# A first piece of 3584 columns with an early store of its own, in a 4-wide L2 pooling kernel

## The chip, the cores and the metric

The kernel runs on one core of a Trainium2 chip. The metric is the device time of one execution in microseconds (us). Three runs of the kernel before gave 394.51, 394.56 and 394.76 us; the median is 394.56 us.

## The reference

The input is `x` of shape 32 x 256 x 4096 in float32. Each run of four neighbours along the last axis becomes one output: the square root of the mean of the four squares.

```python
out_length = length // kernel_size          # 4096 // 4
for i in range(out_length):
    window = np.abs(x[:, :, start:end]) ** p        # p = 2, four elements
    result[:, :, i] = (np.mean(window, axis=-1)) ** (1.0 / p)
```

No output needs anything from another window, so the array can be cut anywhere at a multiple of four. 134.22 MB are read and a quarter of that, 33.55 MB, is written.

## The kernel before, in words

The flat array is seen as 128 partitions of 262144 columns. It is cut into 20 loads: 19 of `W` = 13184 columns (6.75 MB each) and a last one, load 19, of `LAST` = 11648 columns (5.96 MB). The loads are grouped into seven *blocks* (line 50). A block is a contiguous region of `x` and of `out`; inside it each partition owns one contiguous row, so that a store of a block of four loads writes 52736 contiguous bytes per partition.

Three input tiles (`x_tiles`, `X_SLOTS` = 3) are used in turn. All loads are issued by SyncE (SP) at line 83, and load i+3 is issued after the arithmetic on load i, when its tile is free again. The order of all work is written out by hand (`manual_schedule`); each engine runs its instructions in program order.

For loads 0 to 17 the work on a load is done in two halves of 6592 columns:

- ScalarE (ACT) squares the half in place (`square`, line 97).
- VectorE (DVE) adds elements 0, 1 to 2, 3 of each group (`pairs`, line 103), and then the two sums (`fours`, line 107), into a PSUM tile `st`.
- ACT takes the square root with a scale of 1/4 (`root`, line 110) into one of four slots of the output tile `ot`. Slot q holds columns qR to (q+1)R, with R = 3296.

When a block's roots are done, its slots are stored in one DMA (`store`, line 94). The stores of blocks 0 to 3 are issued on ACT's queue from `roots`; those of blocks 4, 5 and 6 are issued on SP's queue, behind all loads. So SP's queue carries all loads and the last three stores. The next roots into `ot` wait for a store of `ot` to land.

The last two loads are handled apart. Load 18 is squared partly by DVE (line 147, columns 0 to 5560) and partly by ACT (the other 7624); DVE then does pairs and fours of both parts, and ACT one root over 3296 results, after which SP stores block 5 (1.69 MB). Load 19 is taken in three pieces with the borders in `ends` (line 153): 6912, 3152 and 1584 columns. ACT's order here is: square of piece 1, root of load 18, square of piece 2, root of piece 1, square of piece 3, root of piece 2, root of piece 3. Only then does SP store block 6 (1.49 MB), the last DMA of the program. The results of loads 18 and 19 lie in the input tile of load 17, which is free by then.

```python
ends = [0, 6912, 10064, LAST]
for a, b in zip(ends, ends[1:]):
    ...
    square(v)
    if a == 0:
        root(place[18], place[18])
        store(5, nc.sync)
```

At the start, a one-column tile `first` is set by DVE and rooted by ACT (lines 121 and 122) while the first load is on its way.

Of the kernel before, what the change touches and what calls it, by code (L numbers as in the profile page):

```python
# [1 line left out]

# [4 lines left out]


@with_exitstack
def kernel(  # L10
    ctx: ExitStack,
    tc: tile.TileContext,
    x: bass.AP,
    p: float,
    kernel_size: int,
    out: bass.AP,
):

    nc = tc.nc

    assert float(p) == 2.0, "kernel specialized for p == 2"
    k = int(kernel_size)  # L30
    assert k == 4, "kernel specialized for kernel_size == 4"

    P = nc.NUM_PARTITIONS
    fp32 = mybir.dt.float32
    Act = mybir.ActivationFunctionType
    add = mybir.AluOpType.add
    xf = x.rearrange("b c l -> (b c l)")
    of = out.rearrange("b c l -> (b c l)")
    total = xf.shape[0] // P

    W = 13184
    H, R = W // 2, W // k
    X_SLOTS = 3
    LAST = total - 19 * W
    widths = [W] * 19 + [LAST]
    n = len(widths)
    assert 0 < LAST <= W and LAST % 16 == 0


    blocks = [[0, 1, 2, 3], [4, 5, 6, 7], [8, 9, 10, 11], [12, 13], [16, 17, 14, 15], [18], [19]]  # L50
    block_of = {i: b for b, loads in enumerate(blocks) for i in loads}
    block_width = [sum(widths[i] for i in loads) for loads in blocks]

    x_pool = ctx.enter_context(tc.tile_pool(name="x_pool", bufs=1))
    o_pool = ctx.enter_context(tc.tile_pool(name="o_pool", bufs=1))
    s_pool = ctx.enter_context(tc.tile_pool(name="s_pool", bufs=1, space=bass.MemoryType.PSUM))
    x_tiles = [x_pool.tile([P, W], fp32, name=f"xt{j}") for j in range(X_SLOTS)]
    o_tile = o_pool.tile([P, 4 * R], fp32, name="ot")
    first = o_pool.tile([P, 1], fp32, name="first")
    s_tiles = [s_pool.tile([P, 2048], fp32, name=f"st{j}") for j in range(2)]  # L60
    ctx.enter_context(tc.manual_schedule())

    def rows(flat, b, div):
        at = sum(block_width[:b]) * P // div
        return flat[at:at + block_width[b] * P // div].rearrange("(p w) -> p w", p=P)


    place = {}
    for b, loads in enumerate(blocks):
        for q, i in enumerate(loads):  # L70
            if i < 18:
                place[i] = o_tile[:, q * R:(q + 1) * R]
    free = x_tiles[17 % X_SLOTS]
    place[18] = free[:, 0:R]
    place[19] = free[:, R:R + LAST // k]

    xs = {}

    def load(i):
        b = block_of[i]  # L80
        at = sum(widths[j] for j in blocks[b][:blocks[b].index(i)])
        xs[i] = x_tiles[i % X_SLOTS][:, 0:widths[i]]
        nc.sync.dma_start(out=xs[i], in_=rows(xf, b, 1)[:, at:at + widths[i]])  # L83

    def store(b, queue):
        if b <= 2:
            held = o_tile[:, :]
        elif b == 3:
            held = o_tile[:, 0:2 * R]
        elif b == 4:  # L90
            held = o_tile[:, :]
        else:
            held = place[blocks[b][0]]
        queue.dma_start(out=rows(of, b, k), in_=held)

    def square(v):
        nc.scalar.activation(out=v, in_=v, func=Act.Square)  # L97

    def pairs(v):

        q = v.rearrange("p (n j) -> p n j", j=k)
        h = v[:, 0:v.shape[1] // 2].rearrange("p (n j) -> p n j", j=2)
        nc.vector.tensor_tensor(out=h, in0=q[:, :, 0:2], in1=q[:, :, 2:4], op=add)  # L103

    def fours(o, v):
        h = v[:, 0:v.shape[1] // 2].rearrange("p (n j) -> p n j", j=2)
        nc.vector.tensor_tensor(out=o, in0=h[:, :, 0], in1=h[:, :, 1], op=add)  # L107

    def root(o, s):
        nc.scalar.activation(out=o, in_=s, func=Act.Sqrt, scale=1.0 / k)  # L110

    def roots(i):
        for c in range(2):
            root(place[i][:, c * R // 2:(c + 1) * R // 2], s_tiles[c][:, 0:R // 2])
        if i in (3, 7, 11, 13):
            store(block_of[i], nc.scalar)

    for i in range(X_SLOTS):
        load(i)

    nc.vector.memset(first[:, :], 1.0)  # L121
    root(first[:, :], first[:, :])
    for i in range(18):
        halves = [xs[i][:, c * H:(c + 1) * H] for c in range(2)]
        waits = i > 1 and (i - 1) % 4 == 0
        square(halves[0])
        if i and not waits:
            roots(i - 1)
        square(halves[1])
        if waits:  # L130
            roots(i - 1)
            for v in halves:
                pairs(v)
            for c, v in enumerate(halves):
                fours(s_tiles[c][:, 0:R // 2], v)
        else:
            for c, v in enumerate(halves):
                pairs(v)
                fours(s_tiles[c][:, 0:R // 2], v)
        if i + X_SLOTS < n:  # L140
            load(i + X_SLOTS)
    roots(17)


    c = 5560
    v = xs[18][:, 0:c]
    nc.vector.tensor_tensor(out=v, in0=v, in1=v, op=mybir.AluOpType.mult)  # L147
    square(xs[18][:, c:W])
    store(4, nc.sync)
    for a, b in ((0, c), (c, W)):  # L150
        pairs(xs[18][:, a:b])
        fours(place[18][:, a // k:b // k], xs[18][:, a:b])
    ends = [0, 6912, 10064, LAST]
    for a, b in zip(ends, ends[1:]):
        v = xs[19][:, a:b]
        o = place[19][:, a // k:b // k]
# [4 lines that stand above are left out]
        pairs(v)  # L161
        fours(o, v)
        if a:
            root(*last)
        last = (o, o)
    root(*last)
    store(6, nc.sync)


# [1 line left out]
_INS = ['x', 'p', 'kernel_size']  # L171
_OUTS = [((32, 256, 1024), 'float32')]

_NUMBERS = {'p': 2.0, 'kernel_size': 4}


# [26 lines left out]
```

## Time and profile before

| What | Value |
|---|---|
| median of three runs | 394.56 us |
| the profiled execution | 394.65 us, span 392.9 us |
| busy, share of the span | ACT 279.3 us (71%), DVE 223.4 us (57%) |
| mean DMA rate over the span | 427 GB/s |
| one load of 6.75 MB, issue to landing | 33.5 us median |
| chain that ended last | DMA 73%, ACT 17%, DVE 6% |

The span is the time from the first to the last instruction of the profiled execution; what lies around it is 394.65 - 392.9 = 1.75 us. The time from issue to landing of a load is twice as long as its transfer since another load usually stands ahead of it in the queue. GpSimd only sets constants, and TensorE is not used.

### The profile page before, as it was taken

To read this page: it belongs to the slowest core of one execution; us is meant where nothing else is said; L and a number is where in the kernel's file an instruction comes from. 1 tells how busy PE (TensorE), PEld (TensorE's weight loads), DVE (VectorE), ACT (ScalarE), POOL (GpSimd) and SP (SyncE) were. 2 spreads that over 40 slices of the span, in tenths; PEclk is the share of its full clock that TensorE was granted. 3 is DMA by queue.
4 is the path that set the end of the run, shared out by engine and by line. 5 is a ranking of instruction groups with operands and counts; after the bars stand their busy time and mean duration, and the time that the engine had idled before them with its cause. 6 is when DMAs were issued, how large, how long until landed. Compare 5 with 4: busy or idle time off the path is not lost.

```text
span 392.9 us, 308 instructions
## 1 busy us (share of the span) xinstructions
DVE 223.4 (57%) x84; ACT 279.3 (71%) x82; POOL 0.2 (0%) x4
## 2 busy tenths in 40 slices
DVE  0046586666460567664515766645066654769992
ACT  1095988987641999877439798774297929897792
POOL 0000000000000000000000000000000000000000
DMA  8999999999999999999999999999999999999997
GB/s 344 430 430 430 435 451 451 435 440 365 430 430 430 446 435 440 435 462 435 430 440 425 430 430 430 430 430 430 435 430 446 427 416 430 430 430 455 415 427 321
DMA packets 3890, 167.79 MB, mean 427 GB/s; under 512 B 432, under 2 KB 432, under 8 KB 432
## 3 DMA queue, kind: packets, MB, share of 16 engines
q1 hardware_dynamic: 3312, 144.15, 85.2%
q10 hardware_dynamic: 576, 23.63, 13.9%
q14 instruction: 2, 0.02, 0.0%
HBM read 134.22 MB, written 33.55 MB: 427 GB/s over the span
## 4 chain that ended last, share of the span: by engine, by line
DMA 73%; ACT 17%; DVE 6%; issue 2%; SPq 0%; ACTq 0%; DVEq 0%
DMA xt<-in_x_dram 46%; DMA out_dram<-ot 27%; ACT xt L97 12%; ACT ot L110 5%; DVE xt L103 3%; DVE st L107 2%; DVE xt L107 1%; ACT xt L110 1%; SPq L83 0%; ACTq L97 0%; ACTq L110 0%; DVEq L103 0%
## 5 line engine op out<-in xcount | busy, mean ns | idle before, releaser
L97 ACT ACTIVATE xt<-xt 128x6592 f32<-128x6592 f32 (+4 forms) x40 | 221.4, 5546 | 63.1 <-DMA xt<-in_x_dram 61.4
L103 DVE TENSOR_TENSOR xt<-xt 128x3296 f32<-128x3296 f32 (+5 forms) x41 | 143.1, 3489 | 126.4 <-ACT xt L97 126.2
L107 DVE TENSOR_TENSOR st<-xt 128x1648 f32<-128x1648 f32 x36 | 67.4, 1882 | 34.8 <-ACT ot L110 32.9
L110 ACT ACTIVATE ot<-st 128x1648 f32<-128x1648 f32 x36 | 53.5, 1535 | 41.9 <-DMA out_dram<-ot 39.1
L107 DVE TENSOR_TENSOR xt<-xt 128x1390 f32<-128x1390 f32 (+4 forms) x5 | 7.3, 1452 | 0.2
L110 ACT ACTIVATE xt<-xt 128x3296 f32<-128x3296 f32 (+3 forms) x4 | 6.0, 1492 | 1.1 <-DVE xt L107 0.9
L147 DVE TENSOR_TENSOR xt<-xt 128x5560 f32<-128x5560 f32 x1 | 5.9, 5944 | 0.0
L110 ACT ACT_TABLE_LOAD x1 | 1.3, 1283 | 0.7 <-PEq L184 0.7
L121 DVE MEMSET first<- 128x1 f32 x1 | 0.1, 59 | 0.8 <-PEq L184 0.8
L110 ACT ACTIVATE first<-first 128x1 f32<-128x1 f32 x1 | 0.2, 203 | 0.0
L184 POOL MEMSET const-bfloat16-1.0<- 128x1 bf16 x1 | 0.1, 101 | 0.0
L184 POOL MEMSET const-uint8-127<- 128x1 uint8 x1 | 0.1, 101 | 0.0
L184 POOL MEMSET const-float32-0.0<- 128x1 f32 x1 | 0.1, 98 | 0.2 <-issue 0.2
L184 POOL MEMSET const-float32-1.0<- 128x1 f32 x1 | 0.1, 98 | 0.0
## 6 DMA issues: line engine op xcount, KB each, us to landing
xt<-in_x_dram SPq DMA_DIRECT2D x19, 6592.0 KB, 33.5
out_dram<-ot ACTq DMA_DIRECT2D x3, 6592.0 KB, 35.3
out_dram<-ot SPq DMA_DIRECT2D x1, 6592.0 KB, 24.8
xt<-in_x_dram SPq DMA_DIRECT2D x1, 5824.0 KB, 25.2
out_dram<-ot ACTq DMA_DIRECT2D x1, 3296.0 KB, 27.8
out_dram<-xt SPq DMA_DIRECT2D x1, 1648.0 KB, 10.4
out_dram<-xt SPq DMA_DIRECT2D x1, 1456.0 KB, 5.8
```

Source lines behind the costliest of these rows:

```text
L97: nc.scalar.activation(out=v, in_=v, func=Act.Square)
L103: nc.vector.tensor_tensor(out=h, in0=q[:, :, 0:2], in1=q[:, :, 2:4], op=add)
L107: nc.vector.tensor_tensor(out=o, in0=h[:, :, 0], in1=h[:, :, 1], op=add)
L110: nc.scalar.activation(out=o, in_=s, func=Act.Sqrt, scale=1.0 / k)
L121: nc.vector.memset(first[:, :], 1.0)
L147: nc.vector.tensor_tensor(out=v, in0=v, in1=v, op=mybir.AluOpType.mult)
L184: nc = _bacc.Bacc("TRN2", target_bir_lowering=False, num_devices=1)
```

## The change

A piece of 3584 columns becomes a block of its own, number 7, at the end of the array. It is loaded ahead of load 0, into the unused slots 2 and 3 of `ot`. DVE squares it (a multiply), adds pairs and fours; ACT takes the root of the 896 results in each partition, which also stand in `ot`, and issues their store on its own queue ahead of its first square. The tile `first` with its memset and root is gone. Load 19 shrinks by the same 3584 columns, from 11648 to 8064, and its three pieces become 4800, 2176 and 1088 columns. The stored block 6 shrinks from 2912 to 2016 results in each partition.

```diff
-    LAST = total - 19 * W
-    widths = [W] * 19 + [LAST]
-    n = len(widths)
+    FIRST = 3584
+    LAST = total - 19 * W - FIRST
+    widths = [W] * 19 + [LAST, FIRST]
+    n = len(widths) - 1
...
-    blocks = [[0, 1, 2, 3], [4, 5, 6, 7], [8, 9, 10, 11], [12, 13], [16, 17, 14, 15], [18], [19]]
+    blocks = [[0, 1, 2, 3], [4, 5, 6, 7], [8, 9, 10, 11], [12, 13], [16, 17, 14, 15], [18], [19], [20]]
...
-    first = o_pool.tile([P, 1], fp32, name="first")
...
+    v = o_tile[:, 2 * R:2 * R + FIRST]
+    o = o_tile[:, 2 * R + FIRST:2 * R + FIRST + FIRST // k]
+    nc.sync.dma_start(out=v, in_=rows(xf, 7, 1))
     for i in range(X_SLOTS):
         load(i)
-
-    nc.vector.memset(first[:, :], 1.0)
-    root(first[:, :], first[:, :])
+    nc.vector.tensor_tensor(out=v, in0=v, in1=v, op=mybir.AluOpType.mult)
+    pairs(v)
+    fours(o, v)
+    root(o, o)
+    nc.scalar.dma_start(out=rows(of, 7, k), in_=o)
...
-    ends = [0, 6912, 10064, LAST]
+    ends = [0, 4800, 6976, LAST]
```

## The prediction

> **What bounds the kernel now.** I read the page's DMA rows first, as the kernel moves 167.8 MB and computes little.
>
> ```profile
> DMA  8999999999999999999999999999999999999997
> GB/s 344 430 430 430 435 451 451 435 440 365 430 430 430 446 435 440 435 462 435 430 440 425 430 430 430 430 430 430 435 430 446 427 416 430 430 430 455 415 427 321
> ...
> q1 hardware_dynamic: 3312, 144.15, 85.2%
> q10 hardware_dynamic: 576, 23.63, 13.9%
> ```
>
> The 16 DMA engines are busy in every slice but the first and last, and the two queues' shares add to 99.1%. q1 carries all loads and the last three stores, q10 ACT's stores. So the bytes set the time, and a change that moves no byte away can gain only at the ends. Next, the end, by windows (length, DVE and ACT busy, clock, DMA share, GB/s):
>
> ```profile
> 382.00:386.00 4.00, 3.09 (x4) 3.09 (x4) 0.00 (x0) 1.00 0.78 333
> 386.00:388.00 2.00, 0.00 (x0) 0.12 (x1) 0.00 (x0) 1.00 1.01 432
> 388.00:390.00 2.00, 0.00 (x0) 0.00 (x0) 0.00 (x0) 1.00 0.96 408
> 390.00:392.00 2.00, 0.00 (x0) 0.00 (x0) 0.00 (x0) 1.00 0.26 111
> ```
>
> The engines work through the end of the arithmetic (just after 386 us) until about 390.5. (333 is an effect of long packets being counted whole; the stretch before has 545.) There is hardly idle DMA time to win. The issues say why:
>
> ```profile
> out_dram<-ot SPq DMA_DIRECT2D x1, 6592.0 KB, 24.8
> ...
> out_dram<-xt SPq DMA_DIRECT2D x1, 1648.0 KB, 10.4
> out_dram<-xt SPq DMA_DIRECT2D x1, 1456.0 KB, 5.8
> ```
>
> Store 4 (issued 359.76) lands at 384.6, store 5 (378.03) at 388.4, store 6 (386.14) at 391.95. They stand end to end in SP's queue behind load 19: the last store is issued only 2.3 us before the one ahead of it lands. Then the timeline of the end, where that issue comes from:
>
> ```profile
> 358.07 5.94 DVE L147 TENSOR_TENSOR xt<-xt 128x5560 f32<-128x5560 f32 x1
> 359.76 0.35 SPq L94 DMA_DIRECT2D out_dram<-ot  x1
> 369.09 5.96 ACT L97 ACTIVATE xt<-xt 128x6912 f32<-128x6912 f32 x1 [2.91 <-DMA xt<-in_x_dram]
> 372.81 2.15 DVE L107 TENSOR_TENSOR xt<-xt 128x1906 f32<-128x1906 f32 x1
> 375.05 2.95 ACT L110 ACTIVATE xt<-xt 128x3296 f32<-128x3296 f32 x1
> 378.03 8.45 SPq L94 DMA_DIRECT2D out_dram<-xt  x2
> 385.58 0.53 ACT L110 ACTIVATE xt<-xt 128x396 f32<-128x396 f32 x1 [0.91 <-DVE xt L107]
> ```
>
> The root of load 18 (375.05) waits for two things that end together: DVE's last fours of load 18 (372.81 + 2.15 = 374.96) and ACT's square of piece 1 (375.05), which waited 2.91 us for load 19. The chain of waits names only the latter. DVE's chain for load 18 is as late, to 0.1 us. That decides the forecast.
>
> **DMA work.** The trace's packet records give, for one engine, 1.947 us for a packet of 52736 bytes, 1.722 for 46592, 0.493 for 13184 and 0.436 for 11648; a line through the ends is 36.8 ns per 1000 bytes and 8 ns. Each DMA gives an engine eight packets. Removed: load 19 and store 6, 8 x (1.722 + 0.436) = 17.26 us. Added: load 19 at 32256 bytes (1.194), the first piece at 14336 (0.535), store 6 at 8064 (0.304), the early store at 3584 (0.139): 8 x 2.172 = 17.38. Net +0.12 us: nothing saved. The last two lie below the smallest packet measured. From below, bytes alone give 0.297 and 0.132; from above, the 11648-byte row gives 0.436, or up to 8 x 0.297 = 2.4 us more for the early store and 1.1 for store 6. I take the line, since the 13184 and 11648 rows lie on it.
>
> The Trainium skill (DMA: Bandwidth & Descriptors, Measured) asks for at least 1 MiB per DMA and lists 341 GB/s there against 425 for 16 MB; this speaks against the change, which makes store 6 1.03 MB and the early one 0.46 MB. The row answers for queued transfers only: 0.436 us is 26.7 GB/s per engine, 427 for 16. At 341 GB/s store 6 would take 3.0 us instead of 2.4, an estimate from that page, and my sum would be 0.6 us higher.
>
> **The start.** The memset and one-element root (0.06 and 0.20 us) go; they lay under the first load (ACT idles till 19.15). The first piece's 1.83 MB land near 7 us (load 0 took from 1.1 to 19.15 for 15.6 us of packets: 4.28 + 2.5). DVE then multiplies 3584 (L147's 5.94 us for 5560, less 1.04 ns per column: 3.9), adds pairs (1792: 2.0) and fours (896: 1.1); the root takes 0.9. The store is issued near 15 us for 0.38 us (ACTq's dearest issue). Queued behind it on ACT is the square of load 0, which lands only at 23.4, so it waits for none of this: cost nothing; without that cover, 8 us. SP issues one more load ahead of loads 0 to 2 (0.33 us), hidden since the first piece keeps the engines busy for 4.3 us. Roots of load 3 overwrite the early results and must wait for that store, some 70 us after its issue; ACT's 6.75 MB store took 36.5 us beside loads, so this is free. If the queue held the small packets back, ACT would wait there, but that needs a delay twice as long as any row.
>
> What does cost: every landing moves by the early packets, 8 x (0.535 + 0.139) = **5.4 us**. ACT and DVE follow landings and store landings through loads 0 to 18 (L97 waits 61.4 us for loads; L110 39.1 for stores), so their whole chain moves by 5.4. Only at load 19 is it given back.
>
> **The end.** Load 19 lands at 369.05 + 5.4 - 8 x (1.722 - 1.194) = 370.2, only 1.2 later. ACT is free at 366.2 + 5.4 = 371.6 (square of 7624 ended 366.18), squares piece 1 (4800: 4.2, at 0.84 ns per column) to 375.8. But DVE ends load 18 at 374.96 + 5.4 = 380.4. Root 18 now waits 4.6 us for DVE. From there, with slopes of the rows (ACT 0.84, DVE 1.04 ns per element, 0.15 to 0.2 us fixed): root 18 2.86 to 383.25; square of 2176 2.0 to 385.25; root of 1200 and square of 1088 2.1 to 387.4; pairs of 544 0.75, fours of 272 0.45, root 0.45: store 6 is issued at **389.1** instead of 386.14. Root 18 comes 5.35 us later (375.05 to 380.4), and the smaller pieces give back 2.4 (8.7 us from root 18 to the issue, in place of 11.1): +3.0.
>
> Store 4 (issued 365.2, before load 19 lands) and store 5 (383.4, before store 4 lands at 385.8) stay seamless, 1.2 later: store 5 lands at 389.6. A landing follows the engine's last packet by 0.45 us (391.51 and 391.96 in the records), so engines run dry between 388.2 and 389.2. Store 6, issued at 389.1, finds them idle: a new gap. No store of before is issued to idle engines; the nearest row is the first load. Its first packet starts 1.03 us after issue: with 2.43 of packets and 0.45, landing at 393.0 is the low end. Its whole surplus over packets, from issue at 0.72 to 19.15, is 2.85: 394.4 is the high end. I take the middle, 393.7, as part of the first load's surplus (first packets 0.7 us too long on average) belongs to the program's start. The last instruction ends 0.9 later: span 394.6, plus 1.75 around it 396.35, less 0.09 by which the profiled run exceeds the median: **396.3 us**, +0.45%. The two ends give 395.6 and 397.0.
>
> **Rivals.** *The queue stays full (not slower).* If store 6 is issued before about 387.5, engines go straight on and the time is 394.56 + 0.12 = 394.7. This decides if the arithmetic moves by 1.4 us or less instead of 3.0, for instance if load 18's chain were tied to something that does not move by 5.4. For it: the chain of waits shows load 19's landing, not DVE, before the final arithmetic, and from 370.2 that chain alone would issue store 6 near 384. Against: DVE ran without a gap from 354.50 to 374.96. Chance 0.14.
>
> *Start-up costs shrink (faster).* First packets run 0.7 us long on average, and 0.85 us on every engine at the first ACT store (near 92 us). If small first packets took both away, everything would be 1.55 earlier: 394.75 with the new gap, 393.1 with a full queue, so faster by over 0.2% needs both. No row shows either cost falling with size. Chance 0.04.
>
> *Small packets are dear (slower still).* With 0.436 us for 3584 bytes, the shift is 7.8, store 6 goes out at 391.5, and its packets may take 1.1 more: 398.7 to 399.8. Against it stands the line through the sizes. Chance 0.05.
>
> *The store is not early:* held till load 0 lands, it would move the same bytes and give the forecast.
>
> **How the numbers follow.** The forecast has 0.77, its own range 395.4 to 397.1. Reaching down to the full queue gives 394.7 to 397.1, which holds about 0.8. A measurement tells about 0.2% (0.8 us) from no change: the bounds are 393.8 and 395.35. Slower takes the forecast and the dear packets, less a little of the forecast's low end: 0.80; same 0.15; faster 0.05.
>
> **What would show it.** Right: the root of 3296 near 380.4 with a wait for DVE L107; store 6 issued near 389 and landing in 4 to 5 us; a DMA dip between 388 and 391; load landings 5.4 later until load 18. Wrong: store 6 issued before 387.5, no dip, or first landings moved by much more or less than 4.3 us.

## The result: 0.27% slower, by a gap of the DMA engines before the last store

The changed kernel takes 395.71 us (median) against 394.59 us for the kernel before, run beside it: a ratio of 1.0027 with a 95% interval from 1.0021 to 1.0034. The profiled execution took 395.33 us with a span of 393.6 us, 0.38 us under its median; it was the fastest of the 22.

The page of the changed kernel, DMA rows first:

```profile
DMA  8999999999999999999999999999999999999996
GB/s 353 434 447 414 445 440 434 429 429 434 423 434 429 429 429 429 434 429 429 429 430 429 429 440 461 435 440 434 434 429 402 429 461 440 429 429 424 424 429 276
...
q1 hardware_dynamic: 3456, 143.69, 84.7%
q10 hardware_dynamic: 720, 24.08, 14.2%
```

By the DMA row all slices but the last are as full as before; the last one falls, from 321 to 276 GB/s. The windows of the end (length, DVE and ACT busy with counts, clock, DMA share, GB/s) show where:

```profile
386.00:388.00 2.00, 1.89 (x4) 1.69 (x3) 0.00 (x0) 1.00 0.88 376
388.00:390.00 2.00, 0.26 (x1) 0.43 (x1) 0.00 (x0) 1.00 0.31 130
390.00:392.00 2.00, 0.00 (x0) 0.00 (x0) 0.00 (x0) 1.00 0.96 399
```

Between 388 and 390 us the engines are busy for 0.31 of the time, where before they had 0.96. They wait for the last store, as the timeline and the issues show:

```profile
363.10 5.94 DVE L153 TENSOR_TENSOR xt<-xt 128x5560 f32<-128x5560 f32 x1
364.67 10.64 ACT L97 ACTIVATE xt<-xt 128x7624 f32<-128x7624 f32 x2
377.85 2.14 DVE L107 TENSOR_TENSOR xt<-xt 128x1906 f32<-128x1906 f32 x1
380.08 2.95 ACT L110 ACTIVATE xt<-xt 128x3296 f32<-128x3296 f32 x1 [4.78 <-DVE xt L107]
383.06 6.03 SPq L94 DMA_DIRECT2D out_dram<-xt  x2
388.30 0.43 ACT L110 ACTIVATE xt<-xt 128x272 f32<-128x272 f32 x1 [0.58 <-DVE xt L107]
```

```profile
out_dram<-xt SPq DMA_DIRECT2D x1, 1648.0 KB, 6.3
out_dram<-xt SPq DMA_DIRECT2D x1, 1008.0 KB, 3.8
```

Root 18 starts 5.0 us later than before and now waits 4.78 us for DVE. Store 5 (issued 383.06) lands at 389.3; store 6 is issued at 388.75, 0.34 us before the end of the merged SPq row, and lands 3.8 us later. In the packet records the engines end store 5 between 387.9 and 388.9 and begin store 6 between 389.6 and 389.7: a gap of 0.7 to 1.8 us. Counted from 375 us to each engine's last packet, the 16 engines idle 1.5 us each on average, against 0.03 us in the kernel before; this is called the idle time per engine below.

### The profile page after: what moved, and what is told of

It is laid out like the page before. It is cut to its first block, busy times and chain, and to the rows that moved or that the text cites. A ratio compares the mean times of both kernels' runs of the same rounds, so it can differ in the third digit from the quotient of the medians.

```text
span 393.6 us, 315 instructions
## 1 busy us (share of the span) xinstructions
DVE 227.5 (58%) x86; ACT 276.2 (70%) x82; POOL 0.2 (0%) x4
## 4 chain that ended last, share of the span: by engine, by line
DMA 67%; ACT 17%; DVE 9%; issue 5%; SPq 0%; ACTq 0%; DVEq 0%
DMA xt<-in_x_dram 40%; DMA out_dram<-ot 27%; ACT xt L97 11%; ACT ot L110 5%; DVE xt L103 4%; DVE st L107 2%; DVE xt L153 1%; ACT xt L110 1%; DVE xt L107 1%; SPq L83 0%; SPq L121 0%; ACTq L94 0%; ACTq L110 0%; ACTq L97 0%; DVEq L103 0%
## 5 line engine op out<-in xcount | busy, mean ns | idle before, releaser
L97 ACT ACTIVATE xt<-xt 128x6592 f32<-128x6592 f32 (+4 forms) x40 | 218.3, 5472 | 50.0 <-DMA xt<-in_x_dram 48.3
L103 DVE TENSOR_TENSOR xt<-xt 128x3296 f32<-128x3296 f32 (+5 forms) x41 | 141.2, 3443 | 116.3 <-ACT xt L97 116.1
L110 ACT ACTIVATE ot<-ot 128x896 f32<-128x896 f32 x1 | 0.9, 949 | 13.4 <-DVE ot L107 13.4
L110 ACT ACTIVATE xt<-xt 128x3296 f32<-128x3296 f32 (+3 forms) x4 | 5.2, 1306 | 5.4 <-DVE xt L107 5.4
L124 DVE TENSOR_TENSOR ot<-ot 128x3584 f32<-128x3584 f32 x1 | 3.9, 3893 | 8.3 <-DMA ot<-in_x_dram 8.3
L107 DVE TENSOR_TENSOR xt<-xt 128x1390 f32<-128x1390 f32 (+4 forms) x5 | 6.3, 1265 | 0.2
L103 DVE TENSOR_TENSOR ot<-ot 128x1792 f32<-128x1792 f32 x1 | 2.0, 2024 | 0.0
L107 DVE TENSOR_TENSOR ot<-ot 128x896 f32<-128x896 f32 x1 | 1.1, 1091 | 0.0
```

## The experiments

**The size of the early piece.** The first kernel halves it.

```diff
-    FIRST = 3584
+    FIRST = 1792
...
-    ends = [0, 4800, 6976, LAST]
+    ends = [0, 5872, 8528, LAST]
```

> The early piece is halved to 1792 columns (early packets of 1792 bytes), load 19 is 9856 columns in pieces of 5872, 2656, 1328. Theory (the whole chain of loads 0 to 18 moves by the early packets, and the last store is then issued to engines that have run dry): everything moves by about 2.4 us, root 18 starts near 377.4, store 6 is issued near 387.2, its first packets start near 388.0 while engines end store 5 between 387.3 and 388.4, so hardly a gap: about 394.6 us, as before (394.4 to 394.9). Rival (small early packets and two more DMAs are what costs): as many DMAs with still smaller packets cost no less than in the changed kernel, 395.7 or more.

Measured: 394.68 us beside 394.65, ratio 1.0001 (0.9992 to 1.0009). The timeline of this kernel:

```profile
377.42 2.95 ACT L110 ACTIVATE xt<-xt 128x3296 f32<-128x3296 f32 x1 [2.97 <-DVE xt L107]
380.39 7.09 SPq L94 DMA_DIRECT2D out_dram<-xt  x2
```

Root 18 is late by half as much, store 6 is issued at 387.14, and store 5 lands at 380.39 + 8.4 = 388.8. The idle time per engine is 0.3 us. As many DMAs with packets half as large cost nothing that can be told (the interval ends at 0.35 us): neither their number nor their small size made the loss.

The second kernel doubles the piece (it then needs slots 1 to 3 of `ot`).

```diff
-    FIRST = 3584
+    FIRST = 7168
...
-    v = o_tile[:, 2 * R:2 * R + FIRST]
-    o = o_tile[:, 2 * R + FIRST:2 * R + FIRST + FIRST // k]
+    v = o_tile[:, R:R + FIRST]
+    o = o_tile[:, R + FIRST:R + FIRST + FIRST // k]
...
-    ends = [0, 4800, 6976, LAST]
+    ends = [0, 2672, 3872, LAST]
```

> The early piece is doubled to 7168 columns (early packets of 7168 bytes), load 19 is 4480 columns in pieces of 2672, 1200, 608. Theory (moved chain, dry engines): the chain moves by about 10.3 us, root 18 starts near 385.3, store 5 itself is issued near 388.3 to engines that ran dry near 386, store 6 near 391.8 follows it without a gap and lands near 395.0: about 398 us (397.5 to 398.7). Rival (small packets and the number of DMAs): larger packets and the same number of DMAs, so 395.7 or a little less.

Measured: 397.87 us, ratio 1.0083 (1.0070 to 1.0096). The profiled execution took 398.59, 0.7 above the median. Its windows and timeline:

```profile
386.00:388.00 2.00, 1.97 (x3) 1.89 (x1) 0.00 (x0) 1.00 0.00 0
388.00:390.00 2.00, 0.37 (x1) 2.00 (x2) 0.00 (x0) 1.00 0.16 66
```

```profile
386.11 2.95 ACT L110 ACTIVATE xt<-xt 128x3296 f32<-128x3296 f32 x1 [6.55 <-DVE xt L107]
389.09 3.90 SPq L94 DMA_DIRECT2D out_dram<-xt  x2
```

Now store 5 is late too: no packet begins between 386 and 388 us. In this execution even store 4 comes late: the first engines have landed load 19 at 369.5, and it is issued at 370.83. The idle time per engine is 2.6 us, and 2.2 more ahead of store 4. Loss against size is 0.0, 1.1 and 3.2 us for 1792, 3584 and 7168 columns. It begins where the arithmetic becomes later than the queue, and is not in proportion to the packets.

**The arithmetic alone, with the early piece kept.** VectorE gets a shorter part of load 18, and ScalarE, which waits there anyway, squares the rest in two parts.

```diff
-    c = 5560
+    c, m = 2400, 7792
...
-    square(xs[18][:, c:W])
+    square(xs[18][:, c:m])
+    square(xs[18][:, m:W])
...
-    for a, b in ((0, c), (c, W)):
+    for a, b in ((0, c), (c, m), (m, W)):
```

> The changed kernel, with the early piece kept, but VectorE multiplies only 2400 columns of load 18, and ScalarE squares the rest in two parts of 5392, so that VectorE's chain on load 18 ends earlier. Theory (VectorE's chain on load 18, moved by 5 us, makes the last store late): root 18 starts near 378.7 instead of 380.1, store 6 is issued near 387.3 and finds engines that have just ended store 5: 394.7 us (394.4 to 395.0), the loss gone with all early packets still there. Rival (the early packets cost DMA time): no change, 395.7.

Measured: 395.03 us beside 394.65, ratio 1.0017 (1.0006 to 1.0028), so by the medians two thirds of the loss are gone (0.38 us are left of 1.12) with all early packets in place. The interval is wide because the runs fall into two groups: eight of the twelve took 394.7 to 395.1, less than any run of the changed kernel, and four 396.0 to 396.5. The profiled execution took 394.74:

```profile
378.83 2.95 ACT L110 ACTIVATE xt<-xt 128x3296 f32<-128x3296 f32 x1 [0.60 <-DVE xt L107]
381.81 6.03 SPq L94 DMA_DIRECT2D out_dram<-xt  x2
```

Store 6 goes out at 387.50, 1.25 us earlier, and the idle time per engine falls from 1.5 to 0.35 us. The median lies just above the range that was expected. What the four slower runs spent, no trace shows.

**The arithmetic alone, without an early piece.** In the kernel before, VectorE multiplies more of load 18.

```diff
-    c = 5560
+    c = 8560
```

> The kernel before, without any early piece, but VectorE multiplies 8560 columns of load 18 instead of 5560, which makes its chain on that load 3.1 us longer. Theory: root 18 starts near 378.1 instead of 375.05, store 6 is issued near 389.2 to engines that ran dry between 387.0 and 388.1, first packets near 390.05, landing near 394.0 instead of 391.95: about 396.6 us (396.2 to 397.2), a loss of the same kind without any early packet. Rival (the early packets cost): VectorE has slack here, no change, 394.6.

Measured: 396.41 us, ratio 1.0046 (1.0033 to 1.0059). Windows and timeline:

```profile
386.00:388.00 2.00, 1.79 (x3) 1.40 (x2) 0.00 (x0) 1.00 0.39 165
388.00:390.00 2.00, 0.26 (x1) 0.53 (x1) 0.00 (x0) 1.00 0.22 93
```

```profile
377.98 2.95 ACT L110 ACTIVATE xt<-xt 128x3296 f32<-128x3296 f32 x1 [3.12 <-DVE xt L107]
380.96 8.22 SPq L94 DMA_DIRECT2D out_dram<-xt  x2
```

The same wait for DVE and the same dip, with no early packet anywhere. Root 18 moved by 2.9 us and the time by 1.8; store 6 had some slack in the queue before. The idle time per engine is 2.6 us.

**The early store held back.** The early sums stay in PSUM; their roots are taken after load 18's square, and their store stands in the queue between stores 5 and 6, where the engines ran dry. (The piece has 3200 columns, since its 800 sums fit the columns of the two `st` tiles that nothing else uses.)

```diff
+    kept = [s_tiles[j][:, R // 2:R // 2 + 400] for j in range(2)]
...
-    nc.scalar.dma_start(out=rows(of, 7, k), in_=o)
...
     store(4, nc.sync)
+    early = free[:, R + LAST // k:R + LAST // k + FIRST // k]
+    for j in range(2):
+        root(early[:, j * 400:(j + 1) * 400], kept[j])
...
             store(5, nc.sync)
+            nc.sync.dma_start(out=rows(of, 7, k), in_=early)
```

> An early piece of 3200 columns whose 800 sums stay in PSUM; their roots are taken only while ScalarE has nothing else to do at the end, and their store (packets of 3200 bytes) is issued on SyncE's queue between stores 5 and 6. Load 19 has 8448 columns in pieces of 5024, 2288, 1136. Theory (the engines run dry before the last store): the chain moves by 3.5 us only, since no early store stands ahead of it, root 18 starts near 378.5, store 6 is issued near 387.3, and the held store keeps the engines busy till then: 394.5 us (394.2 to 394.9). Rival (one more load and store in small packets cost as such): the same number of DMAs and packets of 3200 bytes, so 395.4 to 395.7.

Measured: 394.80 us beside 394.56, ratio 1.0008 (0.9999 to 1.0016): not told from no change. Load 17 landed at 343.19 against 339.65 before, a move of 3.54 us, where the early piece's loads alone were put at 3.5. The timeline:

```profile
378.53 2.95 ACT L110 ACTIVATE xt<-xt 128x3296 f32<-128x3296 f32 x1 [3.74 <-DVE xt L107]
381.50 0.34 SPq L94 DMA_DIRECT2D out_dram<-xt  x1
381.89 0.43 SPq L170 DMA_DIRECT2D out_dram<-xt  x1
387.42 0.33 SPq L94 DMA_DIRECT2D out_dram<-xt  x1
```

The small store (L170, packets of 3200 bytes) lands at 389.3, and store 6 follows; the idle time per engine is 0.2 us. Two things changed at once here, the chain moves by less and the gap has a filler; no run takes them apart.

**Both together.** The held store, and load 18 in three parts as above.

> As the kernel with the held store, and load 18 squared in three parts (2400 columns on VectorE, twice 5392 on ScalarE), so that store 6 is issued earlier still. Theory: the queue is full to the end with or without this, so the bytes set the time: 394.5 us (394.2 to 394.8), no gain over the kernel with the held store beyond 0.3 us, and no clear gain over the kernel before. Rival (the final arithmetic bounds the end): another 1 us less, 393.5.

Measured: 394.74 us, ratio 1.0005 (0.9996 to 1.0014). Store 6 is issued at 386.64, 0.8 us earlier than with the held store alone, for no gain that can be told: the idle time per engine falls only from 0.2 to 0.1 us, and with the queue full to the end earlier arithmetic has nothing more to bring. No version was found that beats the kernel before.

**Columns taken from load 18 instead of load 19.**

```diff
-    LAST = total - 19 * W - FIRST
-    widths = [W] * 19 + [LAST, FIRST]
+    LAST = total - 19 * W
+    W18 = W - FIRST
+    widths = [W] * 18 + [W18, LAST, FIRST]
...
-    c = 5560
+    c = 4048
...
-    ends = [0, 4800, 6976, LAST]
+    ends = [0, 6912, 10064, LAST]
```

> The early piece of 3584 columns with its store on ScalarE's queue as in the changed kernel, but the columns are taken from load 18 (9600 left, 4048 of them squared by VectorE) and load 19 keeps its 11648 in pieces of 6912, 3152, 1584. Theory (what hurts is that VectorE's chain on load 18 moves by 5 us and is not shortened): that chain is now 4.4 us shorter, root 18 (2400 results) starts near 376, store 6 is issued near 386.4 while store 5 still runs: 394.6 us (394.3 to 395.0). Rival (the early packets cost): 395.7.

Measured: 394.90 us, ratio 1.0015 (1.0006 to 1.0023). By the median most of the loss is gone, with the early load and store of 3584 columns as in the changed kernel. The profiled execution took 395.61, 0.7 more than the median, so it is read only for what root 18 waits for:

```profile
370.90 5.96 ACT L98 ACTIVATE xt<-xt 128x6912 f32<-128x6912 f32 x1 [0.42 <-DMA xt<-in_x_dram]
376.77 2.19 ACT L111 ACTIVATE xt<-xt 128x2400 f32<-128x2400 f32 x1
```

(Lines stand one lower here.) Root 18 waits for no one: it follows the square of piece 1, which waits for load 19, as before the change. But load 19 landed at 370.82 here, later than in the changed kernel, store 6 was issued at 387.95, and the idle time per engine was 1.8 us. So this execution has a gap too, here behind a late landing (the lag of the last engine, below). That the runs near the median have a smaller one is argued from their time alone; no trace of one was kept.

**The queue of the early store.** It is issued by SyncE behind loads 0 to 2.

```diff
-    nc.scalar.dma_start(out=rows(of, 7, k), in_=o)
+    nc.sync.dma_start(out=rows(of, 7, k), in_=o)
```

> The changed kernel with its early store issued on SyncE's queue, behind loads 0 to 2, instead of ScalarE's. Theory (only the bytes ahead of loads 3 to 18 count, not when the small store moves): the chain is moved by 5 to 5.4 us by the time of load 18 as before, 395.7 us (395.4 to 396.2). Rival (small packets interleaved with loads from a second queue disturb them): no interleaving, so 1 us less.

Measured: 397.07 us beside 394.56, ratio 1.0068 (1.0051 to 1.0084). Neither side expected this. The mechanism at the end is the same, 1.46 us later:

```profile
346.16 5.70 ACT L97 ACTIVATE xt<-xt 128x6592 f32<-128x6592 f32 x1 [1.44 <-DMA xt<-in_x_dram]
381.54 2.95 ACT L110 ACTIVATE xt<-xt 128x3296 f32<-128x3296 f32 x1 [4.78 <-DVE xt L107]
```

Each DMA has 16 landing events in the trace, one for each engine. For load 17 their median is 343.99 us, 0.2 later than in the changed kernel (343.78); but the last comes at 346.14 instead of 344.68. The last engine is 2.49 us behind the first, where it was 1.07. Whether that belongs to this kernel was asked by two more, one with the small store between loads 1 and 2:

```diff
+    load(0)
+    load(1)
...
-    nc.scalar.dma_start(out=rows(of, 7, k), in_=o)
+    nc.sync.dma_start(out=rows(of, 7, k), in_=o)
+    load(2)
```

> The early store on SyncE's queue again, but between loads 1 and 2 instead of behind load 2. With the store behind load 2, load 17 landed 1.5 us later than in the changed kernel although the median of the 16 engines was only 0.2 us later: one engine was 2.5 us behind the first instead of 1.06. If this lag comes with a small store that stands in the queue of the loads, it is there again: load 17 lands near 346, 396.5 us or more. If it came from that one place or is drawn afresh for each program, the lag is 1 to 1.5 us, load 17 lands near 344.7, and the time is that of the changed kernel, 395.7 us.

and the changed kernel again:

> The changed kernel itself, on the same chip as the kernel with the store between loads 1 and 2, to see how much of the lag of the last engine is the same in another profiled execution: 395.7 us (395.4 to 396.1), load 17 landing near 344.7 with the last engine 1.0 to 1.3 us behind the first.

Measured: 396.71 us, ratio 1.0051 (1.0037 to 1.0064), and 395.71 us, ratio 1.0035 (1.0023 to 1.0047). With the store in SyncE's queue load 17 landed at 346.03, the last engine 2.41 us behind the first; with it in ScalarE's, at 344.77 and 1.05. So the extra time came again with the queue, 1.0 us between these two kernels, and in their profiled executions it is the lag of the last engine: load 17's last landing is 1.3 us later, the median of its 16 landings 0.1. In both kernels with SyncE's queue the lag grows at the small store (from 1.4 us at load 0 to 1.8 or 1.9), after block 1's store (2.1, 2.2) and after block 2's (2.4, 2.5); in the two executions of the changed kernel it shrinks from 1.3 and 1.5 at load 0 to 1.07 and 1.05 at load 17.

But such a lag does not need SyncE's queue. Two of the kernels above, with the early store in ScalarE's queue, have it as well: 2.27 us at load 17 in the one that takes its columns from load 18 (1.64 at load 0), and 2.12 in the doubled piece (0.62 at load 0). Both of these profiled executions took 0.7 us more than their kernel's median. The other kernels with an early piece have 0.95 to 1.37 us. So the lag can differ between executions with the early store in the same queue, and that the queue makes it is not shown; why the two kernels with SyncE's queue are slower stays open.

## Why the prediction was right, and where a term was off

- **Bytes set the time, nothing saved.** Right. The new packets took 1.199, 0.535, 0.305 and 0.140 us against 1.194, 0.535, 0.304 and 0.139. The rival of dear small packets falls with these numbers and with the half-sized piece. The rival of smaller start-up costs needed 1.55 us: the first packets did run less long (0.58 us per engine instead of 0.66), and the first stores gave about 0.2 more (below), which is far too little.
- **The start is free.** Right: ACT still idles 8.08 us before load 0's square (24.41). The first piece landed at 8.25, not near 7, and the early store went out at 16.36 instead of near 15; both had cover. That store landed 20.5 us after its issue, long before anyone needed its place.
- **The chain moves by 5.4 us.** 5.03 measured: load 17 landed at 344.68 against 339.65. (Loads 1 to 4 had moved by 6.0 and load 0 by 5.3, where the sum had 4.3 for the first landing: the early store's first packet came at 20.5, ahead of load 0's last ones, and the last engine lagged 0.45 us more.) The medians of the 16 landings moved by 5.1. The packet records give about 0.2 us of the difference: at the first large store loads and stores lost 0.52 us per engine instead of 0.91, and 0.20 went to the early one.
- **Load 19 gives it back, load 18's chain does not.** Right: load 19 landed at 369.83 (370.2 expected), root 18 started at 380.08 (380.4) after 4.78 us of waiting for DVE (4.6). That this is the cause was shown from both sides: a later chain without the piece loses 1.8 us, and with the piece kept, a shorter chain, a held store, or columns taken from load 18 win most of the loss back by their medians.
- **From root 18 to the issue of store 6**: 8.67 us, 8.7 expected.
- **Store 6 from idle engines: the term that was too large.** Expected 4.6 us, the middle between 3.9 and 5.3; measured 3.80, under the low end. The first packets came 0.85 us after issue, on all engines within about 0.15 us; packets took 2.44; the landing followed by 0.4 to 0.5. The first load's spread of starts and its long first packets, half of which the prediction counted, do not come again at the end. The doubled piece's store 5, also issued to idle engines, agrees: 5.37 us, of which 8 x 0.493 = 3.94 are packets, so 1.4 on top, as for the changed kernel's store 6. So does store 6 of the kernel with more columns on VectorE: 4.85 us, of which 3.49 are packets. With 3.8 instead of 4.6 and 5.03 instead of 5.4 the same sum gives 395.2 for the profiled execution, which took 395.33. For the median it would give 395.1, 0.6 less than the 395.71 measured: the forecast of 396.3 stood as near to the median as it did partly because the typical run spends 0.4 us more than the profiled one, on something that no trace shows.
- The estimate from the Trainium skill's 1 MiB rule (DMA: Bandwidth & Descriptors, Measured) put store 6 at 3.0 us of transfer. The packets took 2.44, even on engines that had been idle. Here the measurement decides (the page's row is for loads issued from GpSimd, this is a store issued by SyncE): the size of that store was no cost, its late issue was.
- **"The store is not early" would cost the same**: not where it was tried. Held to the end, with a piece of 3200 columns, it cost less than the early one, as the chain moved by 3.5 us only and the store stood in the gap. In SyncE's queue, where it lands right behind load 1 or 2, it cost 1.0 to 1.4 us more than in ScalarE's; in the profiled executions this is the lag of the last engine, which the prediction did not know of.

## What to carry to other kernels

Work put ahead of a stream that is bound by DMA moves everything behind it by its own transfer time; look for each chain at the end that does not get this time back, even if the chain of waits names only the other one because the two tie. A smaller last transfer is worth nothing while it stands in a full queue, and it costs as soon as its issue comes later than the engines need it. In this case the early piece did no harm when its store was held back to the end, but it did not gain anything either: in a stream that keeps the queue full to the end, there was nothing to win by an early start.

## What was not expected of the hardware

- The 16 engines do not run level. The last lands behind the first, and work waits for the last: in the changed kernel the square of load 17 starts at 344.71, after the last landing event at 344.68. Apart from loads that land beside a block's store, the distance hardly changes from one such store to the next. For load 17 it is 1.1 us in the kernel before and 0.95 to 2.5 in the others (2.4 and 2.5 with the small store in SyncE's queue, 2.1 and 2.3 in two kernels without it). In three of these four it is one engine, in the fourth two.
- When the engines run dry and start afresh they are level again: store 6's landings lie within 0.18 us in the changed kernel and 0.16 in the one with more columns on VectorE, against 1.1 in the kernel before. By these numbers the gap before store 6 gave back part of its own cost: the changed kernel's engines idle 1.5 us each, and its profiled execution is only 0.7 longer than that of the kernel before; with more columns on VectorE it is 2.6 and 1.7. No run takes this apart.
- A store of 1.03 MB issued to idle engines takes 1.4 us more than its packets, less than the 2.85 of the first load of the program.
